# The first stage of a hybrid decoder layer on eight cores: K and V in groups of eight k-tiles, the weight prefetch held, the constants split

## The chip, the cores and the metric

The kernel runs on the eight cores of one Trainium2 chip. The cores do not talk to each other: each computes 1024 of the 8192 tokens (plus a small overlap) and reads all the weights. The metric is the device time of the slowest core, in microseconds (us). Executions come in two states. In the slow one the cores of one die (cores 0 to 3 or 4 to 7), sometimes of both, show a lower granted clock and the time is some per cent longer. All comparisons below are between fast runs, or between cores of a die that was left alone.

## The reference

One decoder layer: RMSNorm, one wide input projection split into Q, K, V, a pooling input and two gates; sliding-window attention beside multi-scale pooling; an output projection; a gated MLP with a short causal convolution; a gated per-layer embedding. Only the beginning matters here:

```python
h = rms_norm(x, norm_mix_pre[i])        # x: (8192, 4096) float32
z = h @ w_in[i]                         # 4096 -> 12800
q, k, v, u, g_attn, g_pool = jnp.split(z, split_points, axis=-1)   # k and v: 256 columns each
```

The normalisation is one factor per token. The kernel therefore multiplies x with the gain alone, runs the matmuls on that, and applies the factor when it moves results out of PSUM, the memory in eight banks that TensorE writes to.

## The kernel before

The "first stage" computes K and V for a core's 1184 tokens, together with the sum of squares of every token ("statistics"), while x arrives for the first time. x comes in 16 pieces of 1.21 MB: four token slices `s` of 296 tokens, each in four quarters `q` of eight k-tiles (a k-tile is 128 of the 4096 input columns). Three buffers hold the pieces, so a piece is asked for when the piece three before it has been used. For each half piece ScalarE (ACT) squares four k-tiles, VectorE (DVE) multiplies them with the gain into bf16, and TensorE (PE) sums the squares with a matrix of ones. K and V are four chunks `c` of 128 columns, and their weights come in 16 transfers, `wkv[c][q]`. These and all large weights are float32 in HBM and are cast to bf16 by the transfer, so half of what is read lands.

```python
for q in range(4):                       # statistics of slice 0 first
    for hf in range(2):
        stat_step(0, q, hf)()
for s in range(NSL):
    if s + 1 < NSL:                      # those of the next slice as side work
        B.side.extend(stat_step(s + 1, q, hf) for q in range(4) for hf in range(2))
    for c in range(4):                   # one bank after the other, all 32 k-tiles each
        for k in range(NCH):
            O("pe", "matmul", [wkv[c][k // 8].b, h0[k].b], [psB[bk]], ...)
            if k % 15 == 14 and B.side:
                B.side.popleft()()
        ...                              # evacuate bank c on DVE, behind the next chunk
```

Side work (`B.side`) is a queue of small steps of other work; TensorE's loop takes the next one after every so many matmuls.

All later stages take weights from a ring of twelve slots, filled by POOL's queue. It starts as soon as the K/V weights have been issued. After every eighth ring load the same queue also gets a "cast": a transfer from HBM to HBM that rewrites 1 MB (landed) of a later weight matrix as bf16.

```python
def load_next(self):
    ...
    self.O("pool", "dma_start", [cast] if cast else [], [self.wringB[i]], dma=f"wr{i}",
           out=self.wring[i][:, 0:nk * 128], in_=src)
    if self.casting and self.nload % 8 == 0:
        self.cast_next()
```

The helper `O` works out the semaphore waits: an operation waits for the writers of what it reads, and a write (also a partial one) waits for earlier writers of the same buffer.

The softmax here doesn't subtract the row's maximum and nothing guards it: scores larger than these inputs give would overflow.

Of the kernel before, what the change touches and what calls it, by code (L numbers as in the profile page):

```python
# [8 lines left out]
BF16 = mybir.dt.bfloat16  # L9
AF = mybir.ActivationFunctionType  # L10
ALU = mybir.AluOpType
# [153 lines left out]
class Builder:  # L165
# [99 lines left out]
    def load_next(self):  # L265
        if self.nload >= len(self.allslabs):
            return
        wname, off, nk, k0, cast = self.allslabs[self.nload]
        i = self.nload % NS
        self.nload += 1  # L270
        assert cast is None or cast.w, wname
        src = self.dram[wname][off:off + nk * 16384].rearrange("(p m) -> p m", p=128)
        self.O("pool", "dma_start", [cast] if cast else [], [self.wringB[i]], dma=f"wr{i}",
               out=self.wring[i][:, 0:nk * 128], in_=src)
        if self.casting and self.nload % 8 == 0:
            self.cast_next()
# [58 lines left out]
def build_nc():  # L335
# [29 lines left out]
    with st:  # L365
# [19 lines left out]
        psB = B.psB = [Buf(f"ps{i}") for i in range(8)]  # L385


        O("act", "dma_start", [], [constB], partial=True, dma="cst0", out=cf[:], in_=cf_d)
        O("act", "dma_start", [], [constB], partial=True, dma="cst1", out=cb[:], in_=cb_d)
        O("dve", "memset", [], [constB], partial=True, ap=ones_b[:], constant=1.0)  # L390
        O("dve", "memset", [], [constB], partial=True, ap=ones_f[:], constant=1.0)
        O("dve", "memset", [], [constB], partial=True, ap=epst[:], constant=EPS)
        for b in range(8):
            O("dve", "memset", [], [psB[b]], ap=ps[:, b, 240:360], constant=0.0)
        r0 = alloc("r0", [OFF_U + UP + 2], F32)
# [46 lines left out]
        h0 = [alloc(f"h0_{c}", [NK], BF16, shift=4) for c in range(NCH)]  # L442
        xsub = [alloc(f"xs{i}", [8, SL], F32) for i in range(NXS)]
        wkv = [[alloc(f"wkv{c}{q}", [8, 128], BF16) for q in range(4)] for c in range(4)]
        sq = [alloc(f"sq{i}", [4, SL], BF16) for i in range(2)]
        vT = [alloc(f"vT{i}", [NK], BF16) for i in range(2)]
        kz = [alloc(f"kz{i}", [NK], BF16) for i in range(8)]
        va = alloc("va", [10, 576], BF16)
        for t in kz:
            O("pool", "memset", [], [t.b], ap=t.v, constant=0.0)  # L450
        O("pool", "memset", [], [va.b], ap=va.v.rearrange("p a b -> p (a b)"), constant=1.0)

        def load_wkv(c, q):
            off = (16 + c) * D * 128 + q * 8 * 16384
            O("pool", "dma_start", [], [wkv[c][q].b], dma=f"wkv{c}{q}", out=wkv[c][q].v.rearrange("p a b -> p (a b)"),
              in_=B.dram["w_in"][off:off + 8 * 16384].rearrange("(p m) -> p m", p=128))

        def load_x(n):
            if n < 4 * NSL:
                i = n % NXS  # L460
                O("sp", "dma_start", [], [xsub[i].b], dma=f"xs{i}", out=xsub[i].v.rearrange("p a b -> p (a b)"),
                  in_=xs_d[n // 4, n % 4])

        for n in range(NXS):
            load_x(n)
        for c in range(4):
            for q in range(4):
                load_wkv(c, q)
        nsq = [0]

        def stat_step(s, q, hf):

            def run():
                cs = slice(s * SL, (s + 1) * SL)
                bk = (s % 2) * 4 + 3
                xt = xsub[(s * 4 + q) % NXS]
                t = sq[nsq[0] % 2]
                nsq[0] += 1
                O("act", "activation", [xt.b], [t.b], out=t.v, in_=xt.v[:, hf * 4:(hf + 1) * 4, :], func=AF.Square)
                for c8 in range(hf * 4, hf * 4 + 4):  # L480
                    c = q * 8 + c8
                    O("dve", "tensor_scalar", [xt.b, constB], [h0[c].b], partial=True, out=h0[c].v[:, cs],
                      in0=xt.v[:, c8, :], scalar1=gains[:, 0, c:c + 1], scalar2=None, op0=ALU.mult)
                if hf == 1:
                    load_x(s * 4 + q + NXS)
                for c4 in range(4):
                    c = q * 8 + hf * 4 + c4
                    O("pe", "matmul", [t.b, constB], [psB[bk]], partial=c > 0, out=ps[:, bk, 0:SL], lhsT=ones_b[:],
                      rhs=t.v[:, c4, :], start=(c == 0), stop=(c == NCH - 1))
                if (q, hf) == (3, 1):  # L490
                    O("act", "activation", [psB[bk], constB], [r0.b], partial=True, out=r0.v[:, cs],
                      in_=ps[:, bk, 0:SL], func=AF.Ln, scale=1.0 / D, bias=epst[:, 0:1])
                    O("act", "activation", [r0.b], [r0.b], partial=True, out=r0.v[:, cs], in_=r0.v[:, cs], func=AF.Exp,
                      scale=-0.5)
            return run

        for q in range(4):
            for hf in range(2):
                stat_step(0, q, hf)()
        for s in range(NSL):  # L500
            cs = slice(s * SL, (s + 1) * SL)
            if s + 1 < NSL:
                B.side.extend(stat_step(s + 1, q, hf) for q in range(4) for hf in range(2))
            for c in range(4):
                bk = (s % 2) * 4 + c
                for k in range(NCH):
                    O("pe", "matmul", [wkv[c][k // 8].b, h0[k].b], [psB[bk]], partial=k > 0, out=ps[:, bk, 0:SL],
                      lhsT=wkv[c][k // 8].v[:, k % 8, :], rhs=h0[k].v[:, cs], start=(k == 0), stop=(k == NCH - 1))
                    if k % 15 == 14 and B.side:
                        B.side.popleft()()  # L510
                if c < 2:
                    for par in range(2):
                        for jj in range(2):
# [4 lines left out]
                else:  # L518
                    O("dve", "tensor_tensor", [psB[bk], r0.b], [vT[c - 2].b], partial=True, out=vT[c - 2].v[:, cs],
                      in0=ps[:, bk, 0:SL], in1=r0.v[:, cs], op=ALU.mult)  # L520
            B.drain_side()
        O("act", "activation", [constB], [constB], out=esink, in_=esink, func=AF.Exp)
        KT = [(0, 32)] + [(32 + 128 * i, 128) for i in range(9)]
        nb = 0
        for c in range(2):
            for t0, tn in ((0, 1), (1, 5), (6, 4)):
                bk = 6 + nb % 2
                nb += 1
                pb = ps[:, bk, :].bitcast(BF16)
                for i in range(tn):  # L530
                    c0, w = KT[t0 + i]
                    O("pe", "transpose", [vT[c].b, constB], [psB[bk]], partial=i > 0, out=pb[0:w, i * 128:(i + 1) * 128],
                      in_=vT[c].v[:, c0:c0 + w], identity=identb[:])
                w = KT[t0][1]
                O("dve" if c else "act", "tensor_copy" if c else "activation", [psB[bk]], [va.b], partial=True,
                  out=va.v[0:w, t0:t0 + tn, 64:576].rearrange("p t (j d) -> p t j d", j=4)[:, :, 2 * c:2 * c + 2, 0:64],
                  in_=pb[0:w, 0:tn * 128].rearrange("p (t j d) -> p t j d", t=tn, j=2),
                  **({} if c else dict(func=AF.Copy)))
        free(xsub, wkv, sq, vT)


        def rhs_e(k, h):
# [799 lines left out]
```

## Time and profile before

| | us |
|---|---|
| fast runs | 6670.79, 6671.21 (a third: 7118.69, slow) |
| profiled execution, slowest core | 6695.6, mean clock 0.991 |
| PE busy in it | 6561.1 (98%) |
| first K/V matmul | 38.1 |
| K/V ends | 142.7 |
| Q projection starts | 146.3 |

The profiled execution was about 25 us longer than the fast runs; most of that came after this stage.

The kernel is bound by TensorE, but not yet in these 146 us. The windows view of the kernel before (each row: the stretch in us, then busy time and instruction count of each engine, the granted PE clock, the DMA share, and the landed GB/s) shows it:

```profile
...
10.00:20.00 10.00, 0.00 (x0) 0.00 (x0) 0.17 (x1) 3.55 (x3) 10.00 (x13) 1.00 0.99 274
...
40.00:50.00 10.00, 9.59 (x76) 7.12 (x75) 6.28 (x20) 4.09 (x4) 0.00 (x0) 1.00 1.02 286
...
80.00:100.00 20.00, 11.94 (x85) 8.25 (x84) 8.23 (x25) 4.54 (x4) 0.00 (x0) 0.87 1.04 217
100.00:120.00 20.00, 18.64 (x140) 13.53 (x138) 12.48 (x37) 7.66 (x8) 0.00 (x0) 0.96 0.95 238
120.00:140.00 20.00, 19.03 (x150) 14.18 (x148) 7.56 (x19) 3.33 (x5) 0.00 (x0) 1.00 0.01 2
...
```

From 10 us on the DMA engines are full (0.95 to 1.07 over all stretches) up to 120 us and then idle (0.01). The PE timeline of the same core (start, duration, what, count; in brackets the idle time before it and what ended it):

```profile
...
38.14 3.12 PE L144 MATMUL ps<-sb_arena 128*128 128x296 bf16 x15
...
55.67 1.19 PE L144 MATMUL ps<-sb_arena 128*128 128x296 bf16 x8 [2.69 <-DMA sb_arena<-w_in]
60.40 1.64 PE L144 MATMUL ps<-sb_arena 128*128 128x296 bf16 x6 [3.55 <-DMA sb_arena<-w_in]
...
98.18 1.14 PE L144 MATMUL ps<-sb_arena,sb_ones_b 128*128 128x296 bf16 x4 [7.71 <-ACT sb_arena L144]
...
126.07 16.68 PE L144 MATMUL ps<-sb_arena 128*128 128x296 bf16 x130 [0.57 <-DVE sb_arena L144]
...
146.26 3.96 PE L144 MATMUL ps<-sb_arena,sb_wr 128*128 128x344 bf16 x15
```

The first waits for `w_in` are for K/V weights. The long one, 7.71 us before 98.18, is for ScalarE, which had itself waited for an x piece (10.92 us, in the waits of ScalarE). The last 130 K/V matmuls of slice 3, whose x is all in, run without a gap. Undisturbed matmuls of this shape start 0.126 us apart, so the 640 of the stage are 80 us of work.

The DMA view of the kernel before, of the first 150 us, says what filled the engines (queue: packets, MB landed, share of 16 engines' time; then issues by destination with count, KB each and median us to landing). q1 is the x queue; q0 carries all casting transfers, POOL's:

```profile
...
q1 hardware_dynamic: 2304, 19.40, 39.7%
q0 software_dynamic: 4080, 8.39, 38.0%
...
sb_arena<-w_in POOLq DMA_DIRECT2D x16, 256.0 KB, 24.7
sb_wr<-w_in POOLq DMA_DIRECT2D x12, 256.0 KB, 63.1
b_out<-w_out POOLq DMA_DIRECT2D x1, 1024.0 KB, 79.3
...
```

### The profile page before, as it was taken

The numbers are of one execution on the slowest core, as the hardware profiler recorded it, in microseconds if no ns is written. First come the engines' busy times: TensorE is split into PE (matmuls) and PEld (weight loads), VectorE is DVE, ScalarE is ACT, GpSimd is POOL, SyncE is SP. The second block draws the span as 40 slices with busy tenths as digits, with TensorE's granted clock in tenths as the row PEclk, the third lists the DMA queues.
The fourth block names the chain that finished last, engine by engine and source line by source line (L and its number), as shares of the span: only waits on it lengthen the run. The fifth ranks groups of instructions, "written<-read, shape, count | busy, mean of one in ns | idle before, by whom it ended". The sixth has DMA issues, their size and how long they took to land.

```text
span 6695.6 us, 104771 instructions; the slowest of 8 cores (6662.8 to 6695.6 us)
## 1 busy us (share of the span) xinstructions
PE 6561.1 (98%) x41283; PEld 4030.5 (60%) x41283; DVE 1975.1 (29%) x2585; ACT 828.2 (12%) x1248; POOL 1352.8 (20%) x2531
## 2 busy tenths in 40 slices
PE   6999999999999999999999999999999999999996
PEld 4656666666665585866644566665446666544443
DVE  3432311111111125433300133332013333334454
ACT  2550000000001233000000000000000000013311
POOL 1111111111112322311111111111111111233332
PEclk9998999999999999999999999999999999999998
DMA  7557988899887587688899988556875555589885
GB/s 180 82 77 95 116 114 114 117 122 120 116 115 170 158 225 218 176 112 109 110 146 161 156 114 111 77 77 119 163 142 77 77 76 76 138 229 262 236 243 189
DMA packets 377185, 923.25 MB, mean 138 GB/s; under 512 B 49920, under 2 KB 72576, under 8 KB 370944
## 3 DMA queue, kind: packets, MB, share of 16 engines
q0 software_dynamic: 290016, 717.91, 66.2%
q1 hardware_dynamic: 86400, 197.94, 9.5%
q8 instruction: 337, 5.52, 0.3%
q14 instruction: 144, 1.18, 0.1%
q10 hardware_dynamic: 288, 0.70, 0.0%
HBM read 1310.05 MB, written 206.61 MB: 227 GB/s over the span
## 4 chain that ended last, share of the span: by engine, by line
PE 95%; DMA 1%; DVE 1%; ACT 1%; issue 1%; POOL 0%; DVEq 0%; ACTq 0%; SPq 0%; POOLq 0%
PE ps L144 95%; DVE sb_arena L144 1%; ACT sb_arena L144 1%; DMA sb_arena<-w_in 1%; DMA sb_arena<-xs 1%; POOL sb_arena L144 0%; DVEq L143 0%; ACTq L143 0%; ACT L144 0%; DVEq L132 0%; ACT sb_warm L144 0%; SPq L143 0%; POOLq L169 0%
## 5 line engine op out<-in xcount | busy, mean ns | idle before, releaser
L144 PE MATMUL ps<-sb_arena,sb_wr 128*128 128x512 bf16 (+5 forms) x39744 | 6410.8, 323 | 7.5 <-DVE sb_arena L144 4.4
L144 PEld LDWEIGHTS ps<-sb_arena,sb_wr 128*128 128x128 bf16 x39744 | 3890.5, 98 | 2434.0 <-issue 12.8
L144 DVE TENSOR_TENSOR sb_arena<-ps,sb_arena 128x512 f32<-128x512 f32 (+10 forms) x904 | 684.1, 757 | 3995.1 <-PE ps L144 3796.4
L144 ACT ACTIVATE sb_arena<-sb_arena 128x512 f32<-128x512 f32 (+11 forms) x686 | 494.1, 723 | 4627.9 <-DVE sb_arena L144 4511.8
L144 POOL DMA_DIRECT2D sb_wr<-w_up x608 | 322.2, 530 | 1750.5 <-PE ps L144 1679.6
L144 DVE TENSOR_TENSOR sb_arena<-sb_arena 128x512 f32<-128x512 f32 (+8 forms) x545 | 449.6, 837 | 532.6 <-ACT sb_arena L144 503.9
L144 DVE SCALAR_TENSOR_TENSOR sb_arena<-sb_arena,sb_cf 128x1024 f32<-128x1024 f32 (+4 forms) x576 | 593.2, 1031 | 40.8 <-DVE sb_arena L144 0.9
L144 POOL DMA_DIRECT2D sb_wr<-w_in x384 | 205.0, 541 | 1295.7 <-PE ps L144 1295.7
L144 POOL DMA_DIRECT2D sb_wr<-w_down x256 | 135.7, 530 | 666.6 <-PE ps L144 641.7
L144 ACT ACTIVATE sb_arena<-ps 128x512 bf16<-128x512 f32 (+7 forms) x291 | 160.2, 550 | 777.4 <-PE ps L144 770.3
L144 PE MATMUL ps<-sb_arena 128*128 128x296 bf16 (+4 forms) x1216 | 182.0, 267 | 30.4 <-DVE sb_arena L144 17.4
L144 POOL DMA_DIRECT2D sb_wr<-b_out x256 | 137.5, 537 | 339.9 <-PE ps L144 316.4
L144 DVE TENSOR_SCALAR sb_arena<-sb_arena,sb_cf 128x1024 f32<-128x1024 f32 (+3 forms) x320 | 183.5, 602 | 55.5 <-PE ps L144 20.2
L144 POOL DMA_DIRECT2D sb_wr<-b_down x256 | 137.6, 537 | 283.5 <-PE ps L144 251.2
L144 POOL DMA_DIRECT2D sb_wr<-b_pg x256 | 137.6, 537 | 232.2 <-PE ps L144 215.9
L144 PEld LDWEIGHTS ps<-sb_arena 128*128 128x128 bf16 (+1 forms) x1216 | 107.9, 98 | 106.2 <-issue 74.8
L144 POOL DMA_DIRECT2D sb_wr<-b_up x160 | 86.2, 538 | 203.4 <-PE ps L144 190.9
L144 PE MATMUL ps<-sb_arena,sb_ones_b 128*128 128x296 bf16 (+3 forms) x289 | 75.1, 338 | 42.5 <-ACT sb_arena L144 21.4
L144 ACT ACTIVATE sb_arena<-ps,sb_cf 64x386 f32<-64x386 f32 (+3 forms) x112 | 69.8, 624 | 287.1 <-PE ps L144 283.0
L144 ACT ACTIVATE sb_arena<-sb_arena,sb_cf 128x512 bf16<-128x512 f32 (+1 forms) x128 | 90.7, 708 | 0.0
L144 DVE TENSOR_TENSOR sb_arena<-sb_arena,sb_cb 128x512 bf16<-128x512 bf16 (+1 forms) x192 | 64.3, 335 | 65.4 <-ACT sb_arena L144 59.7
L144 POOL DMA_DIRECT2D sb_wr<-w_bp x64 | 33.8, 528 | 194.2 <-PE ps L144 190.6
(31 smaller groups left out, 251.5 us busy)
## 6 DMA issues: line engine op xcount, KB each, us to landing
sb_wr<-w_up POOLq DMA_DIRECT2D x608, 256.0 KB, 4.3
sb_wr<-w_in POOLq DMA_DIRECT2D x384, 256.0 KB, 6.2
sb_wr<-b_out POOLq DMA_DIRECT2D x256, 256.0 KB, 3.0
sb_wr<-b_pg POOLq DMA_DIRECT2D x256, 256.0 KB, 6.5
sb_wr<-w_down POOLq DMA_DIRECT2D x192, 256.0 KB, 6.3
sb_wr<-b_down POOLq DMA_DIRECT2D x192, 256.0 KB, 3.7
sb_wr<-b_up POOLq DMA_DIRECT2D x160, 256.0 KB, 3.8
b_out<-w_out POOLq DMA_DIRECT2D x32, 1024.0 KB, 14.1
```

The source lines that it names most:

```text
L144: inst = getattr(engine, fn[0])(**fn[1])
```

## The change

It has five parts:

1. **Groups.** K/V and statistics advance in 16 groups of eight k-tiles: four banks at once, 32 + 8 matmuls.
2. **Order.** K/V weights are issued by quarter, before POOL's memsets and not behind them.
3. **The hold.** The first ring transfer waits until x piece 13 is in; ring and cast follow in order.
4. **Constants in parts.** Only the gains and a matrix of ones are needed at first; the rest is loaded after group 3.
5. **V transposes** become side work of the first Q chunk.

```diff
-        self.O("pool", "dma_start", [cast] if cast else [], [self.wringB[i]], dma=f"wr{i}",
+        self.O("pool", "dma_start", [cast] if cast else [self.gate] if self.nload == 1 else [], [self.wringB[i]], dma=f"wr{i}",
@@
-        O("act", "dma_start", [], [constB], partial=True, dma="cst0", out=cf[:], in_=cf_d)
-        O("act", "dma_start", [], [constB], partial=True, dma="cst1", out=cb[:], in_=cb_d)
+        O("act", "dma_start", [], [gainB], partial=True, dma="cst0", out=cf[:, 0:192], in_=cf_d[:, 0:192])
+        def load_const():
+            O("act", "dma_start", [], [constB], partial=True, dma="cst1", out=cf[:, 192:CF], in_=cf_d[:, 192:CF])
+            O("act", "dma_start", [], [constB], partial=True, dma="cst2", out=cb[:], in_=cb_d)
@@ (load_x)
+                if n == 4 * NSL - 3:
+                    B.gate = Buf("gate")
+                    B.gate.w = dict(xsub[i].b.w)
@@ (the loop of the stage; prep = squares and gain, stat = statistics, kv = 32 matmuls)
+        prep(0)
+        prep(1)
+        for g in range(4 * NSL):
+            s, q = g // 4, g % 4
+            if q == 3:
+                stat(g)
+            kv(g)
+            if q < 3:
+                stat(g)
+            prep(g + 2)
+            if g == 3:
+                load_const()
+            if q == 3:
+                kv_evac(s)
@@
+        for n in range(6):
+            c, (t0, tn) = n // 3, ((0, 1), (1, 5), (6, 4))[n % 3]
+            B.side.append(v_tiles(n, c, t0, tn))
... (cut: bodies of prep, stat, kv; squares in four buffers and not two; statistics in a bank of the other half)
```

More of the change, by code (lines that the diff above doesn't have):

```diff
@@ L385, in build_nc @@
         psB = B.psB = [Buf(f"ps{i}") for i in range(8)]
-        O("act", "dma_start", [], [constB], partial=True, dma="cst0", out=cf[:], in_=cf_d)
-        O("act", "dma_start", [], [constB], partial=True, dma="cst1", out=cb[:], in_=cb_d)
-        O("dve", "memset", [], [constB], partial=True, ap=ones_b[:], constant=1.0)
+        gainB, onesB = Buf("gain"), Buf("ones")
+        O("act", "dma_start", [], [gainB], partial=True, dma="cst0", out=cf[:, 0:192], in_=cf_d[:, 0:192])
+        O("dve", "memset", [], [onesB], partial=True, ap=ones_b[:], constant=1.0)
+        O("dve", "memset", [], [onesB], partial=True, ap=epst[:], constant=EPS)
         O("dve", "memset", [], [constB], partial=True, ap=ones_f[:], constant=1.0)
-        O("dve", "memset", [], [constB], partial=True, ap=epst[:], constant=EPS)
+        def load_const():
+            O("act", "dma_start", [], [constB], partial=True, dma="cst1", out=cf[:, 192:CF], in_=cf_d[:, 192:CF])
+            O("act", "dma_start", [], [constB], partial=True, dma="cst2", out=cb[:], in_=cb_d)
+            for b in (gainB, onesB):
+                for k, v in b.w.items():
+                    constB.w[k] = max(v, constB.w.get(k, 0))
         for b in range(8):
@@ L444, in build_nc @@
         wkv = [[alloc(f"wkv{c}{q}", [8, 128], BF16) for q in range(4)] for c in range(4)]
-        sq = [alloc(f"sq{i}", [4, SL], BF16) for i in range(2)]
+        sq = [alloc(f"sq{i}", [4, SL], BF16) for i in range(4)]
         vT = [alloc(f"vT{i}", [NK], BF16) for i in range(2)]
@@ L448, in build_nc @@
         va = alloc("va", [10, 576], BF16)
-        for t in kz:
-            O("pool", "memset", [], [t.b], ap=t.v, constant=0.0)
-        O("pool", "memset", [], [va.b], ap=va.v.rearrange("p a b -> p (a b)"), constant=1.0)
-        def load_wkv(c, q):
-            off = (16 + c) * D * 128 + q * 8 * 16384
-            O("pool", "dma_start", [], [wkv[c][q].b], dma=f"wkv{c}{q}", out=wkv[c][q].v.rearrange("p a b -> p (a b)"),
-              in_=B.dram["w_in"][off:off + 8 * 16384].rearrange("(p m) -> p m", p=128))
         def load_x(n):
@@ L462, in load_x @@
                   in_=xs_d[n // 4, n % 4])
+                if n == 4 * NSL - 3:
+                    B.gate = Buf("gate")
+                    B.gate.w = dict(xsub[i].b.w)
         for n in range(NXS):
             load_x(n)
-        for c in range(4):
-            for q in range(4):
-                load_wkv(c, q)
-        nsq = [0]
-        def stat_step(s, q, hf):
-            def run():
-                cs = slice(s * SL, (s + 1) * SL)
-                bk = (s % 2) * 4 + 3
-                xt = xsub[(s * 4 + q) % NXS]
-                t = sq[nsq[0] % 2]
-                nsq[0] += 1
-                O("act", "activation", [xt.b], [t.b], out=t.v, in_=xt.v[:, hf * 4:(hf + 1) * 4, :], func=AF.Square)
-                for c8 in range(hf * 4, hf * 4 + 4):
-                    c = q * 8 + c8
-                    O("dve", "tensor_scalar", [xt.b, constB], [h0[c].b], partial=True, out=h0[c].v[:, cs],
-                      in0=xt.v[:, c8, :], scalar1=gains[:, 0, c:c + 1], scalar2=None, op0=ALU.mult)
-                if hf == 1:
-                    load_x(s * 4 + q + NXS)
+        for q in range(4):
+            for c in range(4):
+                off = (16 + c) * D * 128 + q * 8 * 16384
+                O("pool", "dma_start", [], [wkv[c][q].b], dma=f"wkv{c}{q}", in_=B.dram["w_in"][off:off + 8 * 16384]
+                  .rearrange("(p m) -> p m", p=128), out=wkv[c][q].v.rearrange("p a b -> p (a b)"))
@@ new lines, in build_nc, with prep @@
+        for t in kz:
+            O("pool", "memset", [], [t.b], ap=t.v, constant=0.0)
+        O("pool", "memset", [], [va.b], ap=va.v.rearrange("p a b -> p (a b)"), constant=1.0)
+        def prep(g):
+            if g >= 4 * NSL:
+                return
+            s, q = g // 4, g % 4
+            xt = xsub[g % NXS]
+            for hf in range(2):
+                t = sq[(2 * g + hf) % 4]
+                O("act", "activation", [xt.b], [t.b], out=t.v, in_=xt.v[:, hf * 4:(hf + 1) * 4, :], func=AF.Square)
+            for c8 in range(8):
+                c = q * 8 + c8
+                O("dve", "tensor_scalar", [xt.b, gainB], [h0[c].b], partial=True, out=h0[c].v[:, s * SL:(s + 1) * SL],
+                  in0=xt.v[:, c8, :], scalar1=gains[:, 0, c:c + 1], scalar2=None, op0=ALU.mult)
+            load_x(g + NXS)
@@ L486, in run, with stat @@
+        def stat(g):
+            s, q = g // 4, g % 4
+            bk = (1 - s % 2) * 4
+            for hf in range(2):
+                t = sq[(2 * g + hf) % 4]
                 for c4 in range(4):
                     c = q * 8 + hf * 4 + c4
-                    O("pe", "matmul", [t.b, constB], [psB[bk]], partial=c > 0, out=ps[:, bk, 0:SL], lhsT=ones_b[:],
+                    O("pe", "matmul", [t.b, onesB], [psB[bk]], partial=c > 0, out=ps[:, bk, 0:SL], lhsT=ones_b[:],
                       rhs=t.v[:, c4, :], start=(c == 0), stop=(c == NCH - 1))
-                if (q, hf) == (3, 1):
-                    O("act", "activation", [psB[bk], constB], [r0.b], partial=True, out=r0.v[:, cs],
-                      in_=ps[:, bk, 0:SL], func=AF.Ln, scale=1.0 / D, bias=epst[:, 0:1])
-                    O("act", "activation", [r0.b], [r0.b], partial=True, out=r0.v[:, cs], in_=r0.v[:, cs], func=AF.Exp,
-                      scale=-0.5)
@@ L495, in stat_step @@
-            return run
-        for q in range(4):
-            for hf in range(2):
-                stat_step(0, q, hf)()
-        for s in range(NSL):
+            if q == 3:
+                cs = slice(s * SL, (s + 1) * SL)
+                O("act", "activation", [psB[bk], onesB], [r0.b], partial=True, out=r0.v[:, cs],
+                  in_=ps[:, bk, 0:SL], func=AF.Ln, scale=1.0 / D, bias=epst[:, 0:1])
+                O("act", "activation", [r0.b], [r0.b], partial=True, out=r0.v[:, cs], in_=r0.v[:, cs], func=AF.Exp,
+                  scale=-0.5)
@@ L501, in build_nc, with kv, kv_evac @@
+        def kv(g):
+            s, q = g // 4, g % 4
+            for k in range(q * 8, q * 8 + 8):
+                for c in range(4):
+                    bk = (s % 2) * 4 + c
+                    O("pe", "matmul", [wkv[c][q].b, h0[k].b], [psB[bk]], partial=k > 0, out=ps[:, bk, 0:SL],
+                      lhsT=wkv[c][q].v[:, k % 8, :], rhs=h0[k].v[:, s * SL:(s + 1) * SL], start=(k == 0),
+                      stop=(k == NCH - 1))
+        def kv_evac(s):
             cs = slice(s * SL, (s + 1) * SL)
-            if s + 1 < NSL:
-                B.side.extend(stat_step(s + 1, q, hf) for q in range(4) for hf in range(2))
@@ L504, in build_nc @@
             for c in range(4):
                 bk = (s % 2) * 4 + c
-                for k in range(NCH):
-                    O("pe", "matmul", [wkv[c][k // 8].b, h0[k].b], [psB[bk]], partial=k > 0, out=ps[:, bk, 0:SL],
-                      lhsT=wkv[c][k // 8].v[:, k % 8, :], rhs=h0[k].v[:, cs], start=(k == 0), stop=(k == NCH - 1))
-                    if k % 15 == 14 and B.side:
-                        B.side.popleft()()
                 if c < 2:
@@ L520, in build_nc, with v_tiles, run @@
                       in0=ps[:, bk, 0:SL], in1=r0.v[:, cs], op=ALU.mult)
-            B.drain_side()
+        prep(0)
+        prep(1)
+        for g in range(4 * NSL):
+            s, q = g // 4, g % 4
+            if q == 3:
[6 more added lines that the diff above has]
+                load_const()
+            if q == 3:
+                kv_evac(s)
         O("act", "activation", [constB], [constB], out=esink, in_=esink, func=AF.Exp)
         KT = [(0, 32)] + [(32 + 128 * i, 128) for i in range(9)]
-        nb = 0
-        for c in range(2):
-            for t0, tn in ((0, 1), (1, 5), (6, 4)):
-                bk = 6 + nb % 2
-                nb += 1
+        def v_tiles(n, c, t0, tn):
+            def run():
+                bk = 6 + n % 2
                 pb = ps[:, bk, :].bitcast(BF16)
@@ L531, in build_nc @@
                     c0, w = KT[t0 + i]
-                    O("pe", "transpose", [vT[c].b, constB], [psB[bk]], partial=i > 0, out=pb[0:w, i * 128:(i + 1) * 128],
-                      in_=vT[c].v[:, c0:c0 + w], identity=identb[:])
+                    O("pe", "transpose", [vT[c].b, constB], [psB[bk]], partial=i > 0,
+                      out=pb[0:w, i * 128:(i + 1) * 128], in_=vT[c].v[:, c0:c0 + w], identity=identb[:])
                 w = KT[t0][1]
@@ L538, in build_nc @@
                   **({} if c else dict(func=AF.Copy)))
-        free(xsub, wkv, sq, vT)
+                if n == 5:
+                    free(vT)
+            return run
+        for n in range(6):
+            c, (t0, tn) = n // 3, ((0, 1), (1, 5), (6, 4))[n % 3]
+            B.side.append(v_tiles(n, c, t0, tn))
+        free(xsub, wkv, sq)
         def rhs_e(k, h):
```

## The prediction

> **What bounds the kernel.** TensorE: the page gives PE 6561 of 6696 us (98%). The change touches only the first 146 us, 2.2% of the span; the rest keeps its instructions.
>
> **That stretch now.** In the PE timeline the first statistics matmul runs at 21.1 us, the first K/V matmul at 38.1, K/V ends near 142.7, and the Q projection starts at 146.3. K/V and statistics are 512 + 128 matmuls; undisturbed ones start every 0.126 us, so 80 us of work spread over 122. The windows view shows DMA at 0.95 to 1.07 from 10 to 120 us, then 0.01: the stage is bound by DMA until 120 us, then PE runs dense for the last slice's 17 us. By the DMA view 19.4 MB of x share the engines with 4.2 MB (landed bf16) of K/V weights, 3.1 MB of ring prefetch and a 1.05 MB weight cast; the last two are not needed before 146 us. Counting the float32 read by casting transfers (twice what lands) the rate is 0.33 MB/us (30 to 40 us: 2.34 MB x + 2 x 0.51). With both queues busy x takes two thirds of engine time (68.5 to 33.3%). That agrees with the Trainium skill, "DMA: Bandwidth & Descriptors", section "Queues, rings and completion order": each engine alternates between queues packet by packet.
>
> **What changes.**
> - Ring prefetch and cast, 8.4 MB read or 25 us of DMA, leave the period before x is in.
> - K/V weights are issued at about 1 us instead of 14 (POOL memsets move behind), in order of need.
> - Each group is 40 matmuls, 5.0 us; all four banks advance on whatever k-tiles are in.
> - The constants no longer hold the first operations (ACT to 11.7, DVE to 19.7 us).
> - Added: all four banks finish at once, so the last evacuation (eight of 0.49 and two of 0.47 us, 4.85 us on DVE) is no longer hidden behind K/V. V transposes, now side work after the second k-tile of the Q projection, wait for it: about 3.5 us stall plus 2 us transposes, replacing today's 3.6 us.
>
> **Estimate** by hand-fluid arithmetic from these numbers: the four weight quarters (2.1 MB read each) land near 22, 34, 44 and 54 us and gate groups 0 to 3. From 54 us x (4 to 5 us a group) keeps up with PE (5.0), so 13 groups take about 65 us: K/V ends near 120 us, and the Q projection, counting its V stall, stands as today's would at 126. Gain 20 us, all on the critical path. The gate opens about 94 us, leaving time for almost the full ring. Memory placement later may differ slightly; I expect nothing from it.
>
> **Predicted: 6650 us, 8 in 10 within 6634 to 6668.** Faster by over 2%: 0.01; within 2%: 0.98; slower: 0.01.
>
> **What would show it.** First K/V matmul near 22 us; groups about 10 us apart until 54 us, waiting on weight transfers, then back to back at 5 us; end near 120; no ring transfers before about 90 us; a DVE-released stall of 3 to 4 us just after the first Q matmuls; the same time from there on.
>
> **What would make it wrong.** Weights gating longer; x held by the three buffers, since the refill waits for squares, which wait for the statistics two groups back; ACT blocked by the second constant load waiting for the first; a cold clock in gaps (Trainium skill, "TensorE: Matmul & The Clock Gate", Part 1: about 3.4 us to warm; here the first statistics matmuls took 0.28 us each); a late ring; a slow-state median.

## The result

| | before | after |
|---|---|---|
| fast runs, us | 6670.79, 6671.21, 6671.04 | 6653.25 to 6655.91 (six) |
| median of all six | 6715.73 (three of them above 6700) | 6655.02 |
| first K/V matmul | 38.1 | 23.6 |
| K/V ends, Q starts | 142.7, 146.3 | 125.4, 125.4 |
| first attention matmul | 163.6 | 147.9 |

The ratio of fast runs is 0.9976, 95% interval 0.9959 to 0.9992. (A ratio here is the mean time of one kernel's fast runs over that of the other's of the same rounds, so not quite the ratio of the medians.) In microseconds: the mean of the six runs after is 6654.9, that of the three fast runs before 6671.0, a gain of 16.1.

The windows view after, same columns:

```profile
...
40.00:50.00 10.00, 0.81 (x2) 0.21 (x2) 4.72 (x16) 0.00 (x0) 0.00 (x0) 0.57 1.02 286
50.00:60.00 10.00, 7.58 (x38) 4.91 (x39) 0.00 (x0) 0.25 (x1) 0.00 (x0) 0.58 0.51 90
60.00:80.00 20.00, 20.00 (x161) 15.44 (x159) 11.38 (x34) 9.68 (x11) 0.00 (x0) 1.00 0.60 220
...
100.00:120.00 20.00, 20.00 (x161) 15.44 (x159) 9.42 (x27) 9.81 (x10) 5.12 (x10) 1.00 1.04 210
120.00:140.00 20.00, 16.47 (x119) 11.25 (x117) 5.68 (x13) 2.63 (x6) 0.58 (x2) 0.91 0.89 134
...
```

TensorE is dense from 60 us on (20.00 of 20) and the DMA engines are no longer full: 0.51 at 50 to 60 us, 0.60 at 60 to 80. The PE timeline after:

```profile
...
24.91 5.16 PE L144 MATMUL ps<-sb_arena 128*128 128x296 bf16 x29 [0.43 <-DMA sb_arena<-w_in]
...
31.95 3.81 PE L144 MATMUL ps<-sb_arena 128*128 128x296 bf16 x29 [0.49 <-DMA sb_arena<-w_in]
...
42.45 0.41 PE L144 MATMUL ps<-sb_arena 128*128 128x296 bf16 x1 [5.19 <-DMA sb_arena<-w_in]
47.41 0.41 PE L144 MATMUL ps<-sb_arena 128*128 128x296 bf16 x1 [4.55 <-DMA sb_arena<-w_in]
52.42 6.73 PE L144 MATMUL ps<-sb_arena 128*128 128x296 bf16 x29 [4.60 <-DMA sb_arena<-w_in]
...
125.43 1.03 PE L144 MATMUL ps<-sb_arena,sb_wr 128*128 128x344 bf16 x6
129.99 0.22 PE L144 MATMUL ps<-sb_cb,sb_arena 128*32 128x128 bf16 x1 [3.53 <-DVE sb_arena L144]
130.14 1.89 PE L144 MATMUL ps<-sb_arena,sb_wr 128*128 128x344 bf16 x6
...
```

Group 2 gets its four weight transfers one by one, the first by 37.0 us, the others at 42.4, 47.4 and 52.4; from 52.4 on nothing stops TensorE until K/V ends. Then the new stall: 3.53 us until DVE has emptied bank 6, and behind it six Q matmuls in 1.89 us where six usually take 1.03.

### Where the gain comes from, and that it stays

The first attention matmul is a good mark, since V must be transposed and the first Q chunk finished by then. From there to the end all versions take the same time: in the profiled executions of all versions of the table but the first it is 6503.7 to 6507.7 us on every core. So a microsecond won in this stage is a microsecond of the kernel:

| version | Q starts | first attention matmul | the same, median of the eight cores | mean of fast runs | that mean less the first mark | less than before |
|---|---|---|---|---|---|---|
| before | 146.3 | 163.6 | 162.0 | 6671.0 | 6507.4 |  |
| after | 125.4 | 147.9 | 145.2 | 6654.9 | 6507.0 | 16.1 |
| gate_only | 138.4 | 155.3 | 153.6 | 6662.0 | 6506.7 | 10.5 |
| before_cast_held | 137.6 | 154.5 | 153.4 | 6662.4 | 6507.9 | 8.3 |
| after_no_gate | 140.7 | 162.9 | 160.3 | 6671.5 | 6508.6 | 1.0 |
| no_gate_cast_held | 133.6 | 157.1 | 151.6 | 6661.7 | 6504.6 | 9.1 |
| no_gate_cast_const | 126.1 | 148.6 | 147.7 | 6656.7 | 6508.1 | 13.4 |
| after_old_const | 128.1 | 150.5 | 148.3 | 6659.3 | 6508.8 | 13.2 |
| v_late | 124.5 | 141.8 | 139.1 | 6647.8 | 6506.0 | 21.8 |
| both | 118.6 | 135.9 | 133.8 | 6643.7 | 6507.8 | 25.8 |
| both_const | 118.1 | 135.4 | 132.2 | 6642.6 | 6507.2 | 27.6 |

The first two marks are those of the slowest core of the profiled execution, the median takes all eight cores of it, and times are those of timed fast runs. The column before the last therefore mixes executions; it is there to show that the marks explain the times within 4 us. The cores of one execution differ by 4 to 14 us in this mark, so the median is the steadier one; `both` leaves out one run of 6661.9 in which four cores were 20 us slower than the other four. The versions are explained below.

### The profile page after: what moved, and what is told of

It is laid out like the page before. It is cut to its first block, busy times and chain, and to the rows that moved or that the text cites. A ratio compares the mean times of both kernels' runs of the same rounds, so it can differ in the third digit from the quotient of the medians.

```text
span 6654.2 us, 104718 instructions; the slowest of 8 cores (6648.7 to 6654.2 us)
## 1 busy us (share of the span) xinstructions
PE 6528.7 (98%) x41283; PEld 4021.8 (60%) x41283; DVE 1987.8 (30%) x2585; ACT 827.2 (12%) x1248; POOL 1350.9 (20%) x2531
## 4 chain that ended last, share of the span: by engine, by line
PE 96%; DVE 1%; ACT 1%; issue 1%; DMA 1%; POOL 0%; DVEq 0%; ACTq 0%; POOLq 0%
PE ps L144 96%; DVE sb_arena L144 1%; ACT sb_arena L144 1%; DMA sb_arena<-w_in 1%; POOL sb_arena L144 0%; DVEq L143 0%; ACTq L143 0%; ACT L144 0%; DVEq L132 0%; ACT sb_warm L144 0%; POOLq L169 0%
```

## The experiments

Thirteen variants and a repeat of the changed kernel ran in four submissions, each with the kernel before on the same chip. The means of its fast runs there were 6672.5, 6669.6, 6670.7 and 6670.1, so chips and sessions differ by up to 3.0 us, and the column "less than before" of the table above is taken within a submission. The question is which of the parts made the gain. Theory A is the prediction's: 8.4 MB read by ring prefetch and cast crowded x and K/V weights out, and the hold gave those 25 us of DMA back. Theory B: order, grouping and the early start made it.

### The hold alone, on the kernel before

```diff
-        self.O("pool", "dma_start", [cast] if cast else [], ...
+        self.O("pool", "dma_start", [cast] if cast else [self.gate] if self.nload == 1 else [], ...
+                if n == 4 * NSL - 3: B.gate = Buf("gate"); B.gate.w = dict(xsub[i].b.w)     # in load_x
```

> The kernel before, with one thing added: the ring prefetch and the cast are held until x piece 13 has landed. Theory A (the 8.4 MB of early prefetch and cast are what stretched the stage, as the prediction's list put first): K/V ends 20 to 25 us earlier than 142.7, near 118 to 122, and the time falls by about 16 to 20 us, as much as the whole change. Theory B (order and grouping made the gain, the hold hardly matters): K/V ends within 5 us of 142.7 and the time falls by less than 4 us. Own guess: slice 0 still ends late on its weights, near 65, then 20 + 20 + 17 us, K/V end about 123.

Two fast runs: 6663.1 and 6661.0 (the other four were slow, so no ratio is given). K/V ends at 134.5, 8 us earlier, and 10.5 us of time are won: more than B allows, less than A's number. Slice 0 still ended only at about 72 us, on its last weights.

### The change without the hold

```diff
-        ... [cast] if cast else [self.gate] if self.nload == 1 else [] ...
+        ... [cast] if cast else [] ...
```

> The changed kernel with the hold on the ring prefetch taken out, so prefetch and cast follow the K/V weights in their queue from about 23 us. Theory A: x is slowed by 8.4 MB read, K/V ends near 140 to 145, the gain is gone (time near 6670). Theory B: the prefetch starts on the engines only when the weights are in (57 us), x at two thirds of the engines needs 5.2 us a group against 5.0 on TensorE, and K/V ends within 5 us of 125.4 (time 6654 to 6660).

6669.5 to 6674.6 in four fast runs, ratio to before 0.9998 (0.9983 to 1.0014): the whole gain is gone. K/V ends at 140.7. The PE timeline of this run has two new waits:

```profile
...
81.28 0.66 PE L144 MATMUL ps<-sb_arena,sb_ones_b 128*128 128x296 bf16 x4 [3.25 <-ACT sb_arena L144]
...
102.01 2.13 PE L144 MATMUL ps<-sb_arena,sb_ones_b 128*128 128x296 bf16 x8 [7.58 <-DVE sb_arena L144]
...
140.73 1.03 PE L144 MATMUL ps<-sb_arena,sb_wr 128*128 128x344 bf16 x6
...
```

Theory B falls: without the hold the other parts are worth nothing. But A's account in bytes was not yet proven either, because two things in this trace do not look like bytes. First, the DMA view from 82 to 85 us:

```profile
...
DMA packets 25, 0.40 MB, mean 133 GB/s; under 512 B 2, under 2 KB 4, under 8 KB 9
...
q0 software_dynamic: 16, 0.34, 95.9%
q1 hardware_dynamic: 7, 0.06, 8.0%
...
sb_arena<-xs SPq DMA_DIRECT2D x2, 1184.0 KB, 16.2
```

Only 25 packets moved in 3 us. Sixteen packets of q0 held the engines for 95.9% of the time, which is 46.0 us of engine time (0.959 x 16 x 3). They are of two kinds. By the packet records of this trace ten of them land 32 KB each, the rest 2 KB or less. There are 32 of the large ones in this stage, 1.05 MB together: that is the HBM-to-HBM cast, two packets for each engine. One takes 4.24 us on average, so the cast holds all 16 engines for 8.5 us. K/V and ring packets are short: in the changed kernel from 20 to 30 us, when the K/V weights had the engines nearly alone, 907 packets of q0 landed 1.65 MB with a share of 105.9%, so 0.19 us and 1.8 KB each. The twelve ring transfers are 1536 packets of this kind and hold all 16 engines for 21 us. An x packet takes 0.55 us here (0.080 x 48 / 7).

The 8.0% of x is not yet its share beside the cast, because two of the x pieces were issued only in these 3 us. A cleaner stretch is 92 to 96 us in the kernel before, where two x pieces were on the way all the time (issued at 82.3 and 88.1, landed at 102.9 and 108.5 us) and the cast was moving:

```profile
...
q0 software_dynamic: 42, 0.47, 93.5%
q1 hardware_dynamic: 35, 0.28, 25.0%
...
```

Here x has 25.0% of the engines. Beside ring packets alone (80 to 84 us of the same trace) it has 68.7%, beside K/V packets 66.7% (changed kernel, 40 to 50 us). The Trainium skill, "DMA: Bandwidth & Descriptors", section "Queues, rings and completion order", says that an engine takes turns between queues by whole packets. The counts agree: 274 packets of x to 285 of q0 in the changed kernel from 40 to 50 us, and 35 to 42 above. With turns by packets, the share of a queue depends on the length of its packets.

Second, the queue of ScalarE (the rows ACTq are its DMA issues):

```profile
...
61.39 0.33 ACTq L144 DMA_DIRECT2D sb_cf<-cf  x1
61.61 2.25 ACT L144 ACTIVATE sb_arena<-sb_arena 128x1184 bf16<-128x1184 f32 x2
79.46 0.33 ACTq L144 DMA_DIRECT2D sb_cb<-cb  x1
79.95 4.43 ACT L144 ACTIVATE sb_arena<-sb_arena 128x1184 bf16<-128x1184 f32 x4 [16.08 <-DMA sb_cf<-cf]
...
```

The second constant table is a partial write to the same `constB` as the first, so its issue waits for the first to land, and everything behind it on ScalarE waits as well: the squares of pieces 6 and 7 start at 79.95 and the refills of their buffers follow them (82.35 and 84.5 us). The same page, section "Anatomy of one DMA — SWDGE (gpsimd) path", says that a semaphore wait happens on the issuing sequencer and not in the DMA engines. This trace agrees: the issue at 79.46 and the squares behind it come when the first load has landed. In the changed kernel the same chain is shorter and lies behind another wait:

```profile
...
62.64 0.33 ACTq L144 DMA_DIRECT2D sb_cf<-cf  x1
62.86 2.25 ACT L144 ACTIVATE sb_arena<-sb_arena 128x1184 bf16<-128x1184 f32 x2
71.00 0.34 ACTq L144 DMA_DIRECT2D sb_cb<-cb  x1
71.49 2.27 ACT L144 ACTIVATE sb_arena<-sb_arena 128x1184 bf16<-128x1184 f32 x2 [6.37 <-PE ps L144]
...
```

Its squares at 71.49 were held last by TensorE (6.37 us), and TensorE lost nothing.

### Neither the hold nor the constants in parts

The edit above and that of the next run together:

```diff
-        ... [self.gate] if self.nload == 1 else [] ...
+        gainB = onesB = constB           # and both tables at the start
```

> The changed kernel with neither the hold nor the constants in parts: the grouping, the early and reordered weights and the late V transposes alone. Theory A: time near 6670 or above. Theory B: most of the gain stays, K/V ends at 126 to 134, time 6655 to 6663.

One fast run in six, 6671.1. The profiled execution was slow on one die; on the other the slowest core starts Q at 137.9. Again nothing of the gain is left. With one fast run this is only a support for the run before, and it shows that the chained constants are not the sole cause of the loss, because in this version both tables are loaded at the start and not in the middle of the stage. Against the next run, which differs by the hold alone, it loses 11.8 us to cast and ring together.

### The change with the constants as before

```diff
+        gainB = onesB = constB           # both tables at the start, everything waits for all of it
+        O("act", "dma_start", [], [constB], partial=True, dma="cst0", out=cf[:], in_=cf_d)
+        O("act", "dma_start", [], [constB], partial=True, dma="cst1", out=cb[:], in_=cb_d)
```

> The changed kernel with the constants loaded as before (all of both tables first, everything waits for them, memsets after). The start is later: the first K/V matmul moves from 23.6 to 26 to 30 us. If the third weight quarter (52.4 us) is what gates the stage, that delay is swallowed: K/V end moves by less than 2 us and the time by less than 2 us (6653 to 6657). If the early start counts, K/V end moves by the same 3 to 6 us as the first matmul.

6659.1 to 6659.5 in three fast runs, 4.4 us more than after (2.9 by the gains). The first K/V matmul moves from 23.6 to 25.6 and the third quarter is complete at 55.3 instead of 52.4 us, with Q starting 2.7 us later. So the delay is not swallowed: 0.6 MB of constants in front of the weights push all of them back. Splitting the constants is worth 3 to 4 us (3.1 by the medians of the eight cores).

### The cast alone held

```diff
-        if self.casting and self.nload % 8 == 0:
+        if self.casting and self.nload % 8 == 0 and self.nload > NS:
```

> The changed kernel without the hold, where only the first weight cast (HBM to HBM, 1 MB landed) waits until the first ring slot is loaded again; the twelve ring transfers still go out early. In the run without the hold x crept while the cast was moving (82 to 85 us: 16 cast packets took 96% of all engine time, x got 7 packets). Theory E (the cast is what starves x, not the 6.3 MB of ring prefetch): no wait for x at 92 to 102 us, K/V end 124 to 130 instead of 140.7, time 6654 to 6660. Theory A' (bytes alone: ring 6.3 of 8.4 MB): at least three quarters of the loss stays, K/V end 136 or later, time 6666 or more.

6660.0 to 6663.5 in four fast runs: 9.8 us of the 16.6 that lie between the versions without the hold (6671.5) and with it (6654.9) come back, with the twelve ring transfers, which read three times as much as the cast, still in place. (The expectation counted sixteen cast packets; ten of them were the cast's, see above.) By the medians of the eight cores the first attention matmul comes 8.7 us earlier, about the 8.5 us for which the cast's packets hold the engines. The time lies between the two numbers, nearer to E's. One wait was left:

```profile
...
95.41 2.13 PE L144 MATMUL ps<-sb_arena,sb_ones_b 128*128 128x296 bf16 x8 [5.82 <-DVE sb_arena L144]
...
```

The same edit on the kernel before:

> The kernel before with the same single edit, the first cast a slot later, all else unaltered. Theory E: the x wait of about 10 us at 88 to 98 us goes, K/V end 132 to 137 as in the run with the whole hold (134.5), time 6659 to 6664. Theory A': less than 3 us of gain, time 6668 or more.

6662.7 and 6662.1 (two fast runs; ratio 0.9987, 0.9966 to 1.0009), Q starts at 137.6. That is the whole hold on the kernel before (6662.0, 138.4) but for the 2 us that the submissions differ by. There the ring prefetch cost about 2 us or less (nothing by the medians, 153.4 and 153.6); the cast was the rest.

### And the constants unchained

```diff
-            O("act", "dma_start", [], [constB], partial=True, dma="cst2", out=cb[:], in_=cb_d)
+            cbB = Buf("cb")
+            O("act", "dma_start", [], [cbB], partial=True, dma="cst2", out=cb[:], in_=cb_d)
```

> As the run without the hold but with the cast late (6661.7 us), and the second constant table no longer waits for the first, so ScalarE does not stand behind that load (there: from 65.4 to 75.3 us). If that block is what delays the squares, and with them the x refills that group 10 then waits for: the 5.8 us wait at 89.6 us goes, time 6653 to 6657. If the twelve ring transfers' share of the engines is the cause: the wait stays, time 6660 or more.

6656.8 and 6656.7: 4.9 us less than with the cast alone held, and 1.8 more than after. The wait at 89.6 us shrinks from 5.82 to 1.47, and the two constant loads now go out one behind the other without a gap on ScalarE:

```profile
...
89.83 1.17 PE L144 MATMUL ps<-sb_arena,sb_ones_b 128*128 128x296 bf16 x8 [1.47 <-DVE sb_arena L144]
...
```
```profile
...
61.65 0.33 ACTq L144 DMA_DIRECT2D sb_cf<-cf  x1
61.87 1.17 ACT L144 ACTIVATE sb_arena<-sb_arena 128x1184 bf16<-128x1184 f32 x1
62.01 0.46 ACTq L144 DMA_DIRECT2D sb_cb<-cb  x1
...
68.83 2.27 ACT L144 ACTIVATE sb_arena<-sb_arena 128x1184 bf16<-128x1184 f32 x2 [4.70 <-PE ps L144]
...
```

The loss without the hold thus has three parts. By the means of the fast runs they are 9.8 us for the cast, 4.9 for the chained constants and 1.8 for the ring prefetch; by the gains 8.1, 4.3 and 2.7; by the medians of the first attention matmul over eight cores 8.7, 3.9 and 2.5. (The slowest cores alone would give 5.8, 8.5 and 0.7; in the run with the cast held that core lies 5.4 us behind its median.) So the cast is 8 to 10 us, the chain 4 to 5, and the 6.3 MB of ring prefetch 2 to 3. Each part is measured with the ones before it already removed; another order was not tried. The parts do touch: the first constant load blocked ScalarE's next issue for 18 us beside ring and cast (61.4 to 79.5) and for 12 beside the ring alone (62.9 to 75.3).

### The early issue of the K/V weights undone

```diff
+        for t in kz:                                   # back in front of the weight transfers
+            O("pool", "memset", [], [t.b], ap=t.v, constant=0.0)
+        O("pool", "memset", [], [va.b], ap=va.v.rearrange("p a b -> p (a b)"), constant=1.0)
         for n in range(NXS):
             load_x(n)
-        for t in kz: ...                               # (the same three lines, after the weights)
```

> The changed kernel with the POOL memsets ahead of the K/V weight transfers again, so these are issued at about 14 us instead of 1.6. The first x pieces then come in alone, but the third quarter lands later. If the early issue counts fully: K/V end moves by 8 to 12 us, time 6662 to 6667. If bytes before the third quarter decide (x 0 to 4 would be in by 22 us and the weights then have the engines alone): K/V end moves by 2 to 5 us, time 6656 to 6660.

6662.5 and 6661.3 in two undisturbed runs (the ratio of 0.9996 takes in a third of 6679.8, in which four cores were up to 0.3% slower; the profiled execution is that one). The loss is 7.0 us by the means, between the two expectations. The trace shows less of it: on the undisturbed die the first attention matmul comes 2.6 us later by the median of its cores (148.1 against 145.5), and its longest core took 6655.8. Where the rest of the 7 us goes was not seen. On the undisturbed die the slowest core starts Q at 128.6; its third quarter is complete at 46.9 us, but of its fourth the third transfer comes only at 57.7.

### x held behind the K/V weights

After the change TensorE waits for weights until 52.4 us while x is far ahead. Theory C: x takes two thirds of the engines although it is not what is missing. Theory D: the x flow paces the groups.

```diff
+                hold = [wkv[1][2].b] if n == 3 else [wkv[1][3].b] if n == 4 else [wkv[3][3].b] if n == 5 else []
-                O("sp", "dma_start", [], [xsub[i].b], ...
+                O("sp", "dma_start", hold, [xsub[i].b], ...
```

The changed kernel was run again beside it:

> The changed kernel unaltered, on the same chip as the next three, as their base: time 6653 to 6657 in the fast state, K/V end near 125.4 us.

One fast run, 6654.1.

> The changed kernel, with x pieces 3, 4 and 5 issued only after half of the third, half of the fourth and all of the fourth quarter of the K/V weights have landed. Theory C (after the change the stage is gated by the third weight quarter, because x runs ahead with two thirds of the engines, and from then on TensorE is dense): the third quarter lands near 37 instead of 52, group 3 starts near 47, from where 13 groups take 65 us, K/V end near 113, time 6641 to 6645. Theory D (the x flow with its three buffers is what paces the groups): holding x back makes it worse, K/V end 126 or later, time 6655 or more.

None of the six runs was fast on both dies, so there is no ratio (one of 6704.8 is marked fast, but its die 1 is that slow). Die 0 was undisturbed in all but one: its longest core took 6646.4 to 6647.7 us, against 6654.2 and 6652.2 of the longest cores in the two profiled executions of the changed kernel, and 6651.3 to 6652.9 of the undisturbed dies of `after_again` on the same chip: 5 us less. On that die, the PE timeline:

```profile
...
37.54 3.81 PE L144 MATMUL ps<-sb_arena 128*128 128x296 bf16 x29 [1.08 <-DMA sb_arena<-w_in]
...
46.22 2.23 PE L144 MATMUL ps<-sb_arena,sb_ones_b 128*128 128x296 bf16 x8 [3.87 <-ACT sb_arena L144]
48.24 10.05 PE L144 MATMUL ps<-sb_arena 128*128 128x296 bf16 x64
...
119.36 1.03 PE L144 MATMUL ps<-sb_arena,sb_wr 128*128 128x344 bf16 x6
...
```

The third quarter is complete at 37.5 us instead of 52.4, and Q starts at 119.4 instead of 125.4. C holds, its number was 6 us too good: group 3 waited for its x piece now (3.87 us by way of ScalarE).

### The V transposes later

```diff
+        B.side.extend([lambda: None] * 5)
```

> The changed kernel, with five empty side steps ahead of the V transposes, so that they start after the twelfth k-tile of the Q projection. The 3.5 us wait for the last evacuation and the cold clock after it (1.4 us by the trace: 1.89 and 1.61 us for six matmuls that take 1.03) go: K/V end unchanged near 125, first attention matmul about 5 us earlier than 147.9, time 6648 to 6651. If the stall were hidden somewhere later, the time stays at 6654.

One fast run, 6647.8, 6 us less than the fast run of the changed kernel beside it (7 less than after). The transposes follow Q matmuls that no longer wait:

```profile
...
124.53 5.38 PE L144 MATMUL ps<-sb_arena,sb_wr 128*128 128x344 bf16 x36
129.84 0.23 PE L144 MATMUL ps<-sb_cb,sb_arena 128*32 128x128 bf16 x1
130.00 1.04 PE L144 MATMUL ps<-sb_arena,sb_wr 128*128 128x344 bf16 x6
...
```

From Q's start to the first attention matmul it takes 17.2 us, in the changed kernel 22.5, in the kernel before 17.3 (but with 3.6 us for the transposes ahead of Q, and a cold start of Q behind them: 15 matmuls in 3.96 us, where 36 take 5.38 here).

### Both, and three versions of it

> The two edits together. Theory C: they act in different stretches and add up, K/V end near 113, first attention matmul near 131, time 6636 to 6641. If the earlier K/V end finds the ring not yet loaded (it opens only when x piece 13 is in), PE waits on w_in transfers after the handover and part of the gain is lost, time 6642 or more.

6644.1 and 6643.3, 10.4 us less than the changed kernel beside it (two of three runs marked fast; the third, 6661.9, is left out as said above). The two edits nearly add up: 5 and 6 us alone. The time is in the range of the second branch, but not for its reason: K/V ends at 118.6 and not at 113, as in the run with x held, and the first Q matmuls follow without a wait for `w_in`, so the ring was in time.

> The version with x held behind weights and late V transposes, with x pieces 3 and 4 released a little earlier (after the second and third weight quarter) and piece 5 after half of the fourth, because in the version before group 3 waited 4 to 5 us for x 3. Group 3 starts near 46 instead of 48.7 and the 1.9 us wait before group 5 goes: K/V end 114 to 117, time 6639 to 6643. If the weights just come later by as much, nothing is won: 6643 to 6645.

```diff
+                hold = [wkv[3][1].b] if n == 3 else [wkv[3][2].b] if n == 4 else [wkv[1][3].b] if n == 5 else []
```

6643.3, 6644.2 and 6644.8 (a fourth run of 6672.5 had one die 30 us behind): nothing won. x 3 came earlier and the fourth quarter later, as the second branch of the expectation had it.

> The version with x held behind weights and late V transposes, with the same unchained constants. With the hold on the ring in place the constants land fast (8 us in the changed kernel's trace, hidden behind a wait for TensorE): no change, 6642 to 6645. If the block costs anything there, 1 to 3 us less.

6641.7, 6642.2 and 6643.7; the ratio to before is 0.9958 (0.9936 to 0.9979), 27.6 us by the means of the fast runs. This is the fastest version; the microsecond to `both`, which ran on another chip, is not resolved.

## Why the prediction was right or wrong

The predicted time, 6650, is 5 us below the measured 6655.0, which lies in the stated range. The gain forecast against the fast runs was 21 us and 16.1 came. (The median of the six runs before, 6715.7, has slow runs in it and is no base for this.) The number came out near because it was built from the weight quarters and from 13 groups of 5.0 us on TensorE (65 us forecast, 65 measured, from about 60 to 125.4). The 25 us of the first item of the list do not enter that sum, so its failure did not show in the time.

- **"bound by DMA until 120 us, then PE runs dense"**: right up to about 98 us. From there TensorE waited only 2.3 us until K/V ended, though the DMA engines stayed full until 120. A full DMA share does not show a bound: in the changed kernel it is 1.04 from 100 to 120 us, with TensorE busy for 20.00 of 20.
- **"Ring prefetch and cast, 8.4 MB read or 25 us of DMA, leave the period"**: this step failed. That the hold is needed is right (without it 1.0 us of gain is left, within the noise). That it works by 25 us of DMA time, in proportion to the bytes, is wrong. In its place the runs showed that the 6.3 MB of ring prefetch, three quarters of those bytes, cost 2 to 3 us. The cast, 2.1 MB read, cost 8 to 10, and a chain of constant loads on ScalarE, which is no matter of prefetched bytes, another 4 to 5. Beside the ring's packets of 0.2 us x kept two thirds of the engines; beside the cast's of about 4 us it had a quarter. I carried the two-thirds share, measured beside K/V packets, over to a transfer with other packets.
- **"ACT blocked by the second constant load waiting for the first"** stood only among the risks. The kernel before has the same chain, but at the start; the change itself moved it into the middle of the stage. With the hold it costs 1 to 2 us at most, not resolved (6643.7 with it, 6642.6 without, on two chips); without the hold it is 4 to 5 us.
- **"the four weight quarters ... land near 22, 34, 44 and 54 us"**: this term was mis-sized, and it makes up the missing 5 us. TensorE had the quarters at 24.9, 32.0, 52.4 and before 61 us. x pieces 3 to 6, issued from 25.5 to 38.8 us, took their two thirds while the third quarter was on its way at one transfer in 5 us. K/V ended at 125.4, predicted 120. The run with x held shows that this is worth 5 to 6 us.
- **"about 3.5 us stall plus 2 us transposes, replacing today's 3.6 us"**: the stall measured 3.53, released by DVE. What was left out is the cold clock behind it: 1.89 and 1.61 us for two sets of six matmuls that take 1.03, so 1.4 us. Among the risks stood a cold clock in gaps, by the Trainium skill, "TensorE: Matmul & The Clock Gate", Part 1; it was not applied to the stall that the same prediction had found. The trace agrees with the page in kind. The cold clock does not follow every such stall: in the profiled execution of the run without the hold, cores 3 and 7 show a stall of 3.57 us and the twelve Q matmuls after it start 0.15 us apart, while on the other six cores the first six start 0.28 apart. The sum of this term came out near by luck: Q's start to the first attention matmul took 5.2 us more than before (22.5 against 17.3), forecast 6, because Q starts cold in the kernel before as well.
- **"The constants no longer hold the first operations"**: worth 3 to 4 us by the run with the old constants. **"K/V weights are issued at about 1 us instead of 14"**: worth 7 us by the times of two runs, 3 by the one trace.
- **"the same time from there on"**: right; 6507.4 before and 6507.0 after from the first attention matmul to the end, by the table.

Because the parts hide behind each other they do not add up: alone on the kernel before, the hold gives 8 to 10 us; taken out of the changed one, it costs 15 to 17.

What stays open: the cast's packets were not made shorter by an experiment, only moved away, so that x suffers by their length is argued from the packet counts and from what holding the cast gives back, and not shown by a run in which only the length differs. A rival stays: the 8.5 us for which the cast holds the engines are about what it cost, so its total time may count and not the length of a packet. Against this speaks only that the ring holds them for 21 us and cost 2 to 3; but why x could spare that time was not tested.

## What to carry to other kernels

Before you count the megabytes that a prefetch takes from a critical load, look at how long the packets of each queue hold an engine: here a small HBM-to-HBM transfer with long packets hurt more than a load of three times its size with short ones. When several loads must be in before work can start, let the one that is not missing yet wait for the one that is; two more edits of one line each (x behind the weights, side work behind the evacuation) gave 10 to 11 us here beside the 16 of the whole change. And when a transfer's issue must wait, see to it that it has nothing to wait for (tried here: 4 to 5 us without the hold), or put it on an engine that has nothing else to do (not tried here).

## What the Trainium skill lacked or had wrong

- "DMA: Bandwidth & Descriptors", section "Queues, rings and completion order", gives the turn-taking by packets but not its consequence: beside the packets of an HBM-to-HBM cast (about 4 us each) the x queue had 25% of the engines, beside casting loads into SBUF (0.2 us each) 67 to 69%.
- The same page has no figure for an HBM-to-HBM casting transfer. Here a 1 MB one (landed) held up a stage by 8 to 10 us, and its packets, as the profile counts them, landed 32 KB each, where the page (section "SWDGE vs HWDGE vs iDMA") prefers at most 4096 B to a packet.
- The same page says that waits sit on the issuing sequencer; it does not warn of a compute engine that issues. Here ScalarE stood for 16.08 us before its squares, because the issue of a 193 KB load waited for a 396 KB one.
- "SBUF — State Buffer" describes the port pair that DVE and GpSimd share as an exclusive lock for one instruction. In the changed kernel the first gain multiplication on DVE is in the trace from 10.0 us to the end of POOL's nine back-to-back memsets at 23.3 us (such an operation takes 0.29 us elsewhere), so the lock seems to hold over a row of instructions; the first K/V matmul came at 23.6 us in every version with that order and the constants in parts. The run with the memsets first fits: there the first gain multiplication is in the trace from 9.4 to 14.3 us, and POOL's last memset ends at 14.1. It cost little here, since the last transfer of the first weight quarter came at 24.9. That a lock is the reason, and that it is not handed over between two memsets, is inferred; no run tested this by itself.
